# A causal mask that moves from two GpSimd products to a bfloat16 product in PSUM, in one head group of a two-layer hybrid decoder

## The chip, the cores and the metric

The kernel runs on one core of a Trainium2 chip. TensorE (PE in the rows) does matrix products and transposes, VectorE (DVE) elementwise work and scans, ScalarE (ACT) activations and copies, GpSimd (POOL) elementwise work and the DMAs with indices, SyncE (SP) issues the other DMAs. Each engine takes its instructions in the order in which the built program has them. The metric is the device time of one execution in microseconds, and lower is better.

## The reference

The model has two layers. In each a token mixer with four head groups (A to D, four heads of 64 each) reads one shared projection, and a mixture of experts follows. The change is in group B, stick-breaking attention over 1024 tokens in blocks of 128 queries:

```python
for i in range(S // SB_BLOCK):
    q0 = i * SB_BLOCK
    kl = q0 + SB_BLOCK
    z = jnp.einsum('bqhd,bkhd->bhqk', q[:, q0:kl], k[:, :kl]).astype(F32) * scale
    t_idx = q0 + jnp.arange(SB_BLOCK)[:, None]
    s_idx = jnp.arange(kl)[None, :]
    mask = s_idx < t_idx
    log1m = jnp.where(mask, jax.nn.log_sigmoid(-z), 0.0)
    cs = jnp.cumsum(log1m, -1)
    log_a = jax.nn.log_sigmoid(z) + cs[..., -1:] - cs
    att = jnp.where(mask, jnp.exp(log_a), 0.0)
    outs.append(jnp.einsum('bhqk,bkhd->bqhd', att.astype(v.dtype), v[:, :kl]))
```

Only the last 128 of a block's `kl` keys, the diagonal block, are touched by the mask: there a query sees the keys before it and not itself.

## The kernel before

A layer has four stages: the input projection; the mixers with the output projection; a short end in which the last tiles are normed and routed; and the experts, whose weights stream in from memory. The program's text weaves generators (one for each head group, one for the output projection `outs`), and an automatic scheduler then fixes each engine's order by its own estimates. So a change of one head group's instructions moves the others' too.

Group B is the class `Stick`. One `unit` is one block of 128 queries of one head: 8 blocks, 4 heads and 2 layers make 64 units. Two units (the heads h = 0 and 1 of a pair) are stepped in turn, and three pairs of tiles `z` and `e` go round. A unit does this:

1. TensorE makes the scores in PSUM tile `a`, in pieces of up to 512 keys, with two products for each piece (`sk` and `sq` in the rows), and VectorE copies each piece to `z`, cut at 40 (L574).
2. ScalarE makes exp and then ln(1 + x) of it in `e`.
3. GpSimd multiplies the diagonal block of `e` by a mask of ones and zeros (L579).
4. VectorE sums `e` from the right (the scan, L580) and subtracts it from `z` (L582); ScalarE takes exp of `z`.
5. GpSimd multiplies the diagonal block of `z` by the same mask (L584).
6. TensorE transposes `z` (L148, `cst` is the identity), ScalarE or VectorE copies that to `e`, and the products with the values (`sv`) add into PSUM tile `b`.

At the end of four blocks `head_norm` norms the result `yb` (L551). RWKV (group A) runs in the same stretch; `tl`, `ra`, `mp`, `ya` are its tiles, and its last instruction of a piece is L503. GpSimd also works for it (L392, L412) and for the output projection (L2078, L2140). A helper records all matrix products as L143 and all activations as L160.

Of the kernel before, what the change touches and what calls it, by code (L numbers as in the profile page):

```python
# [12 lines left out]
BF16 = mybir.dt.bfloat16  # L13
# [4 lines left out]
ALU = mybir.AluOpType  # L18
# [4 lines left out]
P = 128  # L23
# [26 lines left out]
def const_table():  # L50
    p = np.arange(P)
    s, t = p[:, None], p[None, :]
    parts = []

    def put(name, a):
        a = np.asarray(a, np.float32)
        b = np.zeros((P, a.shape[1]), np.float32)
        b[:a.shape[0]] = a
        CONST_COLS[name] = (sum(x.shape[1] for x in parts), a.shape[1])
        parts.append(b)  # L60

    put("ident", np.eye(P))
    put("rep64", (p[:, None] % 64 == np.arange(64)[None, :]))
    put("blk64", (s // 64 == t // 64))
    u, v = p[:, None] % 64, np.arange(64)[None, :]
    put("mp4", np.concatenate([u < v, u <= v, u < v, u <= v], 1))
    put("su", s < t)
    put("sl", t < s)
    put("dneg", np.where(t <= s, 0.0, NEG))
    put("mneg", np.where(s <= t, 0.0, -30000.0))  # L70
    put("ep", np.concatenate([np.arange(4)[:, None] == (p[None, :] // 64 + 2 * j) for j in range(2)], 1))
    put("tokid", np.stack([2 * (128 * k + p) + c + 1 for k in range(NT) for c in range(2)], 1))
    put("iota", np.broadcast_to(p[None, :], (P, P)))

    lev = lambda b: (s // (2 * b) == t // (2 * b)) & (s % (2 * b) < b) & (t % (2 * b) >= b)
    put("lev", np.concatenate([lev(1 << l) for l in range(6)], 1))
    return np.concatenate(parts, 1)
# [11 lines left out]


CONSTS = const_table()
NCONST = CONST_COLS["lev"][0]


class K:


    def __init__(self, ctx, tc, nbig, nmed, consts_dram):
        self.tc, self.nc, self.n = tc, tc.nc, 0
        self.ctx = ctx  # L100
        self.bigp = ctx.enter_context(tc.tile_pool(name="big", bufs=nbig))
        self.medp = ctx.enter_context(tc.tile_pool(name="med", bufs=nmed))
        self.cp = ctx.enter_context(tc.tile_pool(name="cp", bufs=1))
        self.sp = ctx.enter_context(tc.tile_pool(name="sp", bufs=2))
        self.ps = ctx.enter_context(tc.tile_pool(name="ps", bufs=1, space=PSUM))
        self.cst = self.cp.tile([P, NCONST], F32, name="cst")
        self.nc.sync.dma_start(self.cst, consts_dram[:, 0:NCONST])
        t = self.big("lev", 768)
        self.nc.sync.dma_start(t, consts_dram[:, NCONST:NCONST + 768])
        self.lev = self.cp.tile([P, 768], BF16, name="levb")  # L110
        self.nc.vector.tensor_copy(self.lev, t)
        self.evn, self.pe = 0, 0.0
        self.mode, self.mode_load, self.mode_acts = None, None, []
# [440 lines left out]
class Stick:  # L554


    def __init__(self, k, pc):
        self.k, self.pc = k, pc
        self.qk, self.y, self.done = {}, {}, set()

    def unit(self, i, h, py, own):
        k, nc = self.k, self.k.nc
        V, G = nc.vector, nc.gpsimd
        hs = slice(64 * (h % 2), 64 * (h % 2) + 64)
        q, kt = self.qk[i // 4, h // 2]
        q = q[:, 512 * (h % 2) + 128 * (i % 4):512 * (h % 2) + 128 * (i % 4) + 128]
        kl = 128 * (i + 1)
        z, e = own
        for o in range(0, kl, 512):
            n = min(512, kl - o)  # L570
            pz = k.psum("a", n)
            k.mm(pz, q, kt[h % 2][0][:, o:o + n], stop=False)
            k.mm(pz, q, kt[h % 2][1][:, o:o + n], start=False)
            V.tensor_scalar(z[:, o:o + n], pz, 40.0, None, op0=ALU.min)  # L574
        k.act(e[:, :kl], z[:, :kl], AF.Exp)
        k.act(e[:, :kl], e[:, :kl], AF.Ln, bias=1.0)
        yield
        dg = slice(kl - 128, kl)
        G.tensor_tensor(e[:, dg], e[:, dg], k.c("sl"), op=ALU.mult)  # L579
        V.tensor_tensor_scan(e[:, :kl][:, ::-1], e[:, :kl][:, ::-1], e[:, :kl][:, ::-1], initial=0.0,  # L580
                             op0=ALU.add, op1=ALU.bypass)
        V.tensor_tensor(z[:, :kl], z[:, :kl], e[:, :kl], op=ALU.subtract)  # L582
        k.act(z[:, :kl], z[:, :kl], AF.Exp)
        G.tensor_tensor(z[:, dg], z[:, dg], k.c("sl"), op=ALU.mult)  # L584
        yield
        at = e
        for o in range(0, kl, 512):
            n = min(512, kl - o)
            pt = k.psum("a", n)
            for b in range(n // 128):  # L590
                k.tr(pt[:, 128 * b:128 * b + 128], z[:, o + 128 * b:o + 128 * b + 128])
            k.ev(at[:, o:o + n], pt)
        if not py:
            py.append(k.psum("b", 128))
        for b in range(i + 1):
            k.mm(py[0][hs], self.v[:, b, hs], at[:, 128 * b:128 * b + 128],
                 start=b == 0, stop=b == i)
        yield
# [1018 lines left out]
class Trunk:  # L1617
# [12 lines left out]
    def setup(self):  # L1630
        k, nc, ins = self.k, self.nc, self.ins
        V, G, cp = nc.vector, nc.gpsimd, k.cp
        cr = k.big("crow", 128)
        G.memset(cr, 0.0)
        nc.scalar.dma_start(cr[0:8], ins["c"].rearrange("o (n p) -> (o n) p", p=P))
        self.raw = k.big("prow", 128)
        G.memset(self.raw, 0.0)
        for l in range(L_LAYERS):
            for n, cnt in PARAM_ROWS:
                src = ins[PARAM_IN[n]][l]  # L1640
                src = src.rearrange("t (n p) -> (t n) p", p=P) if n == "cw" else src.rearrange("(n p) -> n p", p=P)
                o = 64 * l + PARAM_OFF[n]
                nc.gpsimd.dma_start(self.raw[o:o + cnt], src)

        pt = k.psum("b", 128)
        k.tr(pt, cr)
        cs = k.small("cs", 16, bufs=1)
        k.act(cs[:, 0:8], pt[:, 0:8], AF.Sigmoid)
        V.tensor_tensor(cs[:, 8:16], cs[:, 0:8], pt[:, 0:8], op=ALU.mult)
        self.cz = cp.tile([P, 8, 32], F32, name="cz")  # L1650
        G.memset(self.cz, 0.0)
        V.tensor_copy(self.cz[:, :, 0], cs[:, 8:16])
        self.eps = k.eps = cp.tile([P, 2], F32, name="eps")
        G.memset(self.eps[:, 0:1], 1e-6)
        G.memset(self.eps[:, 1:2], 64e-5)
        self.rst = cp.tile([P, S], BF16, name="rst")
        G.memset(self.rst, 1.0)
        self.one = cp.tile([P, P], F32, name="one")
        G.memset(self.one, 1.0)
        G.memset(self.rst.rearrange("p (c l) -> p c l", l=64)[:, :, 0], 0.0)  # L1660
        self.sums = cp.tile([P, 2, P], BF16, name="sums")
        V.tensor_copy(self.sums[:, 0], k.c("su"))
        G.memset(self.sums[:, 1], 1.0)
        self.idb = cp.tile([P, P], BF16, name="idb")
        V.tensor_copy(self.idb, k.c("ident"))
        self.mneg4 = cp.tile([P, 4, P], BF16, name="mneg4")
        V.tensor_copy(self.mneg4, k.c("mneg").unsqueeze(1).to_broadcast([P, 4, P]))
        self.zd = cp.tile([P, 256], F32, name="zd")
        G.memset(self.zd[:, 0:128], 0.0)
        V.tensor_copy(self.zd[:, 128:256], k.c("dneg"))  # L1670
# [276 lines left out]
    def layer(self, l):  # L1947
        k, nc, ins = self.k, self.nc, self.ins
        pc = self.pc(l)
# [30 lines left out]
            yield from ds.scores()  # L1980
            yield from ds.search()

        sb = Stick(k, pc)
        sb.eps = self.eps[:, 0:1]
        stage = set()
        until = lambda f: iter(lambda: None if f() else WAIT, None)
# [204 lines left out]
```

## Time and profile before

| | us |
|---|---|
| median of 3 runs | 3679.66 (3675.84 to 3692.8) |
| the profiled execution, its time | 3683.57 |
| the profiled execution, its span on the core | 3681.8 |
| TensorE busy in the span | 3226.8 (88%) |
| VectorE busy | 2779.7 (75%) |
| ScalarE busy | 1934.4 (53%) |
| GpSimd busy | 845.3 (23%) |

The span runs from the first to the last instruction; the time lies 1.8 us above it. Busy is the time in which an engine works on an instruction. A share over the whole span is a mean over stages with different limits, so it says little of one stage.

### The profile page before, as it was taken

Reading aid. Unit: us, or ns where it says so; the run is one execution under the profiler, and the core shown is the slowest. Engines: PE = TensorE matmul, PEld = TensorE weight load, DVE = VectorE, ACT = ScalarE, POOL = GpSimd, SP = SyncE. Lnnn points to the kernel's source line nnn. Section 1 sums busy time; section 2 is a strip of 40 time slices with the busy share of each in tenths; the row PEclk is TensorE's granted clock in tenths of the full one; section 3 lists DMA queues with packets and bytes.
Section 4 is the critical chain, followed back from the end, with each engine's and each line's share of the span. In section 5 each row is a group of like instructions: output and inputs, shape, how many; then the busy total and the mean of one; then the engine's idle time right before and its main releaser. Section 6 shows DMA issues by size and latency. Waiting matters only on the chain. (4 is left out here: it accounts for less than half of the span.)

```text
span 3681.8 us, 54634 instructions
## 1 busy us (share of the span) xinstructions
PE 3226.8 (88%) x18838; PEld 2535.1 (69%) x18848; DVE 2779.7 (75%) x5556; ACT 1934.4 (53%) x3324; POOL 845.3 (23%) x769
## 2 busy tenths in 40 slices
PE   6888889998888799999958888999888879999995
PEld 3876645576677678777757866767667667877773
DVE  4589843557766899999856997555776679999994
ACT  4456332234444567777753663433444456777773
POOL 3220110113322113322312102011332211432220
PEclk8989999999988899999979989989998889999997
DMA  5222355533434899999931233023343389999995
GB/s 195 76 85 89 117 192 193 170 125 99 134 115 154 273 371 381 381 382 387 341 110 58 90 97 101 14 76 125 101 132 115 137 282 366 381 382 382 388 347 167
DMA packets 373670, 746.60 MB, mean 203 GB/s; under 512 B 44234, under 2 KB 108384, under 8 KB 373392
## 3 DMA queue, kind: packets, MB, share of 16 engines
q1 hardware_dynamic: 346880, 672.03, 50.9%
q0 software_dynamic: 20256, 70.33, 7.3%
q8 instruction: 149, 2.44, 0.3%
q10 hardware_dynamic: 6256, 0.74, 0.1%
q14 instruction: 129, 1.06, 0.1%
HBM read 635.45 MB, written 107.53 MB: 202 GB/s over the span
## 5 line engine op out<-in xcount | busy, mean ns | idle before, releaser
L160 ACT ACTIVATE wh<-wr 128x1024 fp32r<-128x1024 f32 (+3 forms) x900 | 887.4, 1005 | 328.1 <-DMA wr<-in_moe_w_dram 162.8
L1529 DVE TENSOR_TENSOR wl<-wr,wh 128x1024 fp32r<-128x1024 f32 x792 | 938.1, 1222 | 67.9 <-ACT wh L160 58.8
L143 PE MATMUL pj<-wl,xh 128*128 128x512 f32 x1056 | 419.5, 404 | 15.4 <-DVE wl L1529 14.8
L143 PE MATMUL pj<-wh,xh 128*128 128x512 f32 x1056 | 422.2, 401 | 9.0 <-ACT xh L160 8.4
L143 PE MATMUL pj<-wh,xl 128*128 128x512 f32 x1056 | 420.2, 398 | 0.0
L143 PEld LDWEIGHTS pj<-wl,xh 128*128 128x128 f32 x1056 | 200.1, 190 | 84.4 <-DVE wl L1529 41.1
L143 PEld LDWEIGHTS pj<-wh,xh 128*128 128x128 f32 x1056 | 200.1, 190 | 54.8 <-ACT xh L160 11.0
L143 PEld LDWEIGHTS pj<-wh,xl 128*128 128x128 f32 x1056 | 200.7, 190 | 46.8 <-DVE xl L1541 1.7
L1428 POOL DMA_INDIRECT xg<-h2d,si x64 | 76.6, 1198 | 632.1 <-PE a L148 370.3
L143 PE MATMUL b<-wh,hh 128*128 128x512 f32 x528 | 211.3, 401 | 10.7 <-ACT wh L160 9.1
L143 PE MATMUL pj<-hh,wh 128*128 128x512 f32 x480 | 197.1, 411 | 14.7 <-ACT wh L160 5.7
L143 PE MATMUL b<-wh,hl 128*128 128x512 f32 x528 | 209.2, 396 | 0.0
L143 PE MATMUL pj<-hh,wl 128*128 128x512 f32 x480 | 195.9, 408 | 7.7 <-DVE wl L1845 7.7
L143 PE MATMUL pj<-wh,hh 128*128 128x256 f32 (+2 forms) x640 | 187.2, 305 | 16.9 <-DVE stl L1962 11.5
L143 PE MATMUL pj<-wh,hl 128*128 128x256 f32 (+2 forms) x640 | 192.7, 303 | 3.2 <-DVE hl L1822 3.2
L143 PE MATMUL pj<-hl,wh 128*128 128x512 f32 x480 | 194.1, 404 | 0.0
L143 PE MATMUL pj<-wl,hh 128*128 128x256 f32 (+2 forms) x640 | 189.0, 298 | 2.5 <-POOL wl L1845 2.5
L160 ACT ACTIVATE ra<-b 128x256 f32<-128x256 f32 x192 | 73.2, 383 | 216.1 <-PE b L143 213.8
L143 PE MATMUL b<-wl,hh 128*128 128x512 f32 x528 | 176.8, 411 | 2.2 <-DVE wl L1529 2.1
L1498 POOL DMA_INDIRECT xs<-yo,si x32 | 146.8, 4588 | 124.9 <-DVE yo L1495 111.0
L1498 POOL DMA_INDIRECT out_dram<-yo,si x32 | 136.3, 4259 | 135.7 <-DVE yo L1495 117.1
L421 DVE TENSOR_TENSOR tl<-pj,tl 128x512 f32<-128x512 f32 x128 | 87.1, 685 | 94.7 <-PE pj L143 93.8
(523 smaller groups left out, 7794.5 us busy)
## 6 DMA issues: line engine op xcount, KB each, us to landing
wr<-in_moe_w_dram SPq DMA_DIRECT2D x792, 512.0 KB
aw<-in_ada_w_dram SPq DMA_DIRECT2D x96, 512.0 KB
wr<-in_w_in_dram SPq DMA_DIRECT2D x84, 256.0 KB
wo<-in_w_out_dram SPq DMA_DIRECT2D x48, 256.0 KB
xs<-xp SPq DMA_DIRECT2D x48, 256.0 KB
xp<-xs SPq DMA_DIRECT2D x48, 256.0 KB
out_dram<-xp SPq DMA_DIRECT2D x48, 256.0 KB
sk<-pt SPq DMA_DIRECT2D x32, 256.0 KB
```

What stands on the lines that cost most here:

```text
L143: return self.nc.tensor.matmul(out, lhsT, rhs, start=start, stop=stop, skip_group_check=True)
L160: i = self.nc.scalar.activation(out, in_, f, **kw)
L421: V.tensor_tensor(tt, pT, tt, op=ALU.add)
L1428: self.k.nc.gpsimd.indirect_dma_start(out=xg, out_offset=None, in_=self.h2d, in_offset=bass.IndirectOffsetOnAxis(ap=gi.bitcast(U32), axis=0))
L1498: k.nc.gpsimd.indirect_dma_start(out=self.xs, out_offset=bass.IndirectOffsetOnAxis(ap=si.bitcast(U32), axis=0), in_=yo, in_offset=None, co ...
L1529: i = nc.vector.tensor_tensor(wl, raw, wh.bitcast(F32), op=ALU.subtract)
```

## The change

A constant `low`, 0 where a query may see a key and -30000 elsewhere, takes the place of the mask of ones and zeros. It is cast to bfloat16 once at the start. In each unit a third product, `low` as the weights against a bfloat16 identity, adds it to the diagonal block of the scores while they are in PSUM. Behind exp, ln(1 + x), the sum and the second exp the masked places are then 0 by themselves, and both GpSimd products are gone.

```diff
-    put("sl", t < s)
+    put("low", np.where(s < t, 0.0, -30000.0))
...
             k.mm(pz, q, kt[h % 2][0][:, o:o + n], stop=False)
-            k.mm(pz, q, kt[h % 2][1][:, o:o + n], start=False)
+            last = o + n == kl
+            k.mm(pz, q, kt[h % 2][1][:, o:o + n], start=False, stop=not last)
+            if last:
+
+                k.mm(pz[:, n - 128:], self.low, self.idb, start=False)
             V.tensor_scalar(z[:, o:o + n], pz, 40.0, None, op0=ALU.min)
         k.act(e[:, :kl], z[:, :kl], AF.Exp)
         k.act(e[:, :kl], e[:, :kl], AF.Ln, bias=1.0)
         yield
-        dg = slice(kl - 128, kl)
-        G.tensor_tensor(e[:, dg], e[:, dg], k.c("sl"), op=ALU.mult)
         V.tensor_tensor_scan(e[:, :kl][:, ::-1], e[:, :kl][:, ::-1], e[:, :kl][:, ::-1], initial=0.0,
                              op0=ALU.add, op1=ALU.bypass)
         V.tensor_tensor(z[:, :kl], z[:, :kl], e[:, :kl], op=ALU.subtract)
         k.act(z[:, :kl], z[:, :kl], AF.Exp)
-        G.tensor_tensor(z[:, dg], z[:, dg], k.c("sl"), op=ALU.mult)
         yield
...
+        self.low = cp.tile([P, P], BF16, name="low")
+        V.tensor_copy(self.low, k.c("low"))
...
-        sb = Stick(k, pc)
+        sb = Stick(k, pc, self.low, self.idb)
```

The scheduler makes a new order of it. The first place is TensorE's order at the first units of layer 0; before, the scores of two units stood together:

```order
L143 MATMUL a_7584<-sk_7567,sq_7566 128x128 x2
L143 MATMUL a_7618<-sk_7574,sq_7566 128x128 x2
L148 MATMUL a_7642<-cst,z_7560 128x128
L143 MATMUL b_7645<-e_7561,sv_7581 64x128
L143 MATMUL b_7647<-tl_4464 128x128 x2
```

The same place of the change:

```order
L143 MATMUL a_7586<-sk_7569,sq_7568 128x128 x2
L143 LDWEIGHTS low
L143 MATMUL a_7586<-idb,low 128x128
L143 MATMUL a_7621<-sk_7576,sq_7568 128x128 x2
L143 LDWEIGHTS low
L143 MATMUL a_7621<-idb,low 128x128
L148 MATMUL a_7642<-cst,z_7562 128x128
```

Each unit has a load of weights and a product more, and nothing else changes place here. In 62 of the 64 units the new product stands directly behind the scores; in the other two a few other products lie between.

The second place is TensorE's order around the last two units of layer 0 (block 7, the last two heads): first before, from the last transpose of the pair ahead of them.

```order
L148 MATMUL a_10211<-cst,z_7562 128x128
L143 MATMUL b_10106<-rp_10036,st_9807 64x64 x2
L143 MATMUL a_10239<-sk_9710,sq_9709 128x512
L143 MATMUL a_10239<-sk_9711,sq_9709 128x512
...
L143 MATMUL b_10117<-ya_7433,cst 128x256
L143 MATMUL b_10122<-sqh_10120,cst 128x256
L143 MATMUL b_10128<-gd_7190,lw_291 128x256
L143 MATMUL b_10173<-e_7561,sv_9726 64x128 x7
L143 MATMUL b_10173<-e_7563,sv_9726 64x128 x7
L143 MATMUL b_10195<-wr_304,h2t_10181 128x36 x8
```

And the same place of the change, where `wr` and `h2t` are the router's product, and `sqh`, `gd` are of RWKV's output:

```order
L148 MATMUL a_10198<-cst,z_7564 128x128 x3
L143 MATMUL b_10096<-sqh_10094,cst 128x256
L143 MATMUL b_10102<-gd_7192,lw_293 128x256
L143 MATMUL b_10145<-e_7563,sv_9731 64x128 x7
L143 MATMUL b_10145<-e_7565,sv_9731 64x128 x4
L143 MATMUL b_10167<-wr_306,h2t_10153 128x36 x8
L143 MATMUL b_10145<-e_7565,sv_9731 64x128 x3
L143 MATMUL a_10211<-sk_9715,sq_9714 128x512
L143 MATMUL a_10211<-sk_9716,sq_9714 128x512
```

The scores of the last two units stood ahead of the 14 value products of the pair before them and now stand behind these and the router's product.

The third place is ScalarE's order at these last two units; before, they work in `z_7564` and `z_7560`:

```order
L160 ACTIVATE e_7565<-z_7564 128x1024
L160 ACTIVATE e_7565<-e_7565 128x1024
L160 ACTIVATE sqh_10120<-ya_7433 128x256
L160 ACTIVATE sqh_10120<-b_10122,eps 128x256
...
L160 ACTIVATE sqh_10120<-sqh_10120 128x256
...
L160 ACTIVATE e_7561<-z_7560 128x1024
```

The same place of the change, where they work in `z_7566` and `z_7562`:

```order
L160 ACTIVATE sqh_10094<-b_10096,eps 128x256
L160 ACTIVATE sqh_10094<-sqh_10094 128x256
...
L160 ACTIVATE e_7567<-z_7566 128x1024
L160 ACTIVATE e_7567<-e_7567 128x1024
L160 ACTIVATE e_7563<-z_7562 128x1024
L160 ACTIVATE e_7563<-e_7563 128x1024
```

The second unit's first exp stood behind three activations of RWKV's output and now follows the first unit's directly.

## Rows read from the trace of the kernel before

**Rows 1.** Busy time by stretch: start:end in us, length, then each engine's busy us.

```profile
core 0: us, PE busy (x) PEld busy (x) DVE busy (x) ACT busy (x) POOL busy (x), PEclk, DMA share, GB/s
828.00:1146.00 318.00, 270.01 (x2233) 216.73 (x2232) 223.85 (x407) 145.91 (x319) 93.02 (x120) 0.91 0.38 114
2578.00:2901.00 323.00, 270.42 (x2217) 218.87 (x2216) 225.95 (x406) 144.77 (x317) 95.64 (x119) 0.90 0.37 113
```

**Rows 2.** L503 (RWKV) and L551 (Stick), 828 to 1200: min/median/max ns, first and last start.

```profile
L503 DVE TENSOR_TENSOR ya<-sqh,b x5: 389/412/422, 895.9 to 1128.6; 128x256 f32<-128x256 f32 x5
L551 DVE SCALAR_TENSOR_TENSOR yb<-yb,prm,sqh x4: 744/752/1252, 900.0 to 1144.6; 128x512 f32<-128x512 f32 x4
```

**Rows 3.** GpSimd's two groups with the mask: busy us, mean ns, idle before.

```profile
L584 POOL TENSOR_TENSOR z<-z,cst 128x128 f32<-128x128 f32 x64 | 41.9, 656 | 130.0 <-ACT z L160 130.0
L579 POOL TENSOR_TENSOR e<-e,cst 128x128 f32<-128x128 f32 x64 | 31.7, 499 | 180.3 <-ACT e L160 153.6 <-DMA sq<-pt 26.6
```

**Rows 4.** Who waited for these two lines, whole span: us in total, times.

```profile
  DVE e L580: 13.8, 23
  PEld b L143: 1.5, 2
  PEld a L148: 19.1, 12
  PE a L148: 16.7, 12
```

**Rows 5.** Timeline around 2643 us: start, us, instruction, idle before it and releaser.

```profile
2642.87 0.30 ACT L160 ACTIVATE e<-e 128x128 f32<-128x128 f32 x1
...
2643.25 0.46 POOL L579 TENSOR_TENSOR e<-e,cst 128x128 f32<-128x128 f32 x1 [0.51 <-ACT e L160]
...
2643.74 1.48 DVE L580 TENSOR_TENSOR_SCAN e<-e 128x128 f32<-128x128 f32 x1 [0.39 <-POOL e L579]
```

**Rows 6.** Waits of DVE, then of PE, 828 to 1146: us in total, times, longest.

```profile
DVE e L580 <- POOL e L579: 7.7, 12, 1.7
...
PE a L148 <- POOL z L584: 8.4, 6, 6.1
```

**Rows 7.** Wide and narrow weight loads and products of TensorE: min/median/max ns, or mean.

```profile
L143 PEld LDWEIGHTS <-idb x16: 95/96/253, 653.1 to 2562.5; 128*128 128x128 bf16 x16
L143 PE MATMUL a<-sk,sq 128*128 128x128 f32 x32 | 6.9, 278 | 1.0 <-ACT yc L160 0.7
```

**Rows 8.** VectorE's scan and difference by shape: busy us, mean ns.

```profile
L580 DVE TENSOR_TENSOR_SCAN e<-e 128x128 f32<-128x128 f32 x8 | 7.6, 946 | 2.4 <-POOL e L579 2.4
L580 DVE TENSOR_TENSOR_SCAN e<-e 128x256 f32<-128x256 f32 x8 | 6.4, 804 | 0.9 <-POOL e L579 0.9
L582 DVE TENSOR_TENSOR z<-z,e 128x768 f32<-128x768 f32 x8 | 9.5, 1191 | 0.0
L582 DVE TENSOR_TENSOR z<-z,e 128x896 f32<-128x896 f32 x8 | 8.5, 1077 | 0.0
```

**Rows 9.** Timeline of the last two units of layer 0.

```profile
1118.32 0.33 PE L148 MATMUL a<-cst,z 128*128 128x128 f32 x1
...
1119.61 0.69 DVE L574 TENSOR_SCALAR z<-a 128x512 f32<-128x512 f32 x1 [0.96 <-PE a L143]
...
1122.05 0.69 DVE L574 TENSOR_SCALAR z<-a 128x512 f32<-128x512 f32 x1
...
1122.35 1.06 ACT L160 ACTIVATE e<-e 128x1024 f32<-128x1024 f32 x1
...
1125.02 2.89 PE L143 MATMUL b<-e,sv 128*64 128x128 f32 x28
...
1126.80 1.06 ACT L160 ACTIVATE e<-z 128x1024 f32<-128x1024 f32 x1 [0.88 <-PE b L143]
...
1127.84 1.98 PE L143 MATMUL b<-wr,h2t 128*128 128x36 f32 x16
...
1136.05 1.09 PE L148 MATMUL a<-cst,z 128*128 128x128 f32 x8
```

More of the change, by code (lines that the diff above doesn't have):

```diff
@@ L554, with __init__ @@
 class Stick:
-    def __init__(self, k, pc):
+    def __init__(self, k, pc, low, idb):
         self.k, self.pc = k, pc
+        self.low, self.idb = low, idb
         self.qk, self.y, self.done = {}, {}, set()
@@ L562, in unit @@
         k, nc = self.k, self.k.nc
-        V, G = nc.vector, nc.gpsimd
+        V = nc.vector
         hs = slice(64 * (h % 2), 64 * (h % 2) + 64)
```

## The prediction

> **What bounds the kernel now.** I read the busy time by stretch first, to find where group B works and which engine is nearest its limit there. Group B's 64 units run in two stretches, one for each layer, of 318 and 323 us. In them TensorE works 270 us of each, VectorE some 225, ScalarE some 145, GpSimd 93 to 96 [rows 1]. So no engine is full: TensorE is at 84 to 85%, and the rest is waits between engines that each take their instructions in a fixed order. GpSimd is far from a limit, so what it is relieved of is worth nothing as work. It can only be worth something as a wait.
>
> Next I read when the two streams of the stretch end. In layer 0 the last norm of group B starts at 1144.6, the last piece of RWKV at 1128.6 [rows 2]. Group B ends last, so a shorter group B can shorten the stretch. All before and behind it (projection, norms, experts) is the same work and moves with the end.
>
> Then the two mask lines by themselves and who waited for them. They are 128 products, 73.6 us of GpSimd in all, 0.46 to 0.66 us each [rows 3]. Waits that end at them: VectorE's scan 23 times, 13.8 us; TensorE's transposes 12 times, 16.7 us (19.1 us seen from the weight loads, which is the same wait); a product with values twice, 1.5 us [rows 4]. So of 128 products only some 37 were waited for at all. The other 91 were hidden, since their consumer was held up by something else or had other work ahead.
>
> **The change, part by part.**
>
> *The two GpSimd products go.* What one costs the waiting engine I take from the timeline: ScalarE's ln ends at 2643.17 (2642.87 and 0.30), GpSimd runs from 2643.25 to 2643.71, and the scan starts at 2643.74 [rows 5]. A direct hand-over from ScalarE to VectorE stays and costs about the 0.08 us that ScalarE to GpSimd took. That leaves at most 0.49 us for each wait.
>
> - Scan: 23 waits of at most 0.49 us would be 11.3 us. The mean wait is 0.6, but the longest is 1.7 [rows 6], so others are shorter than 0.49. I take 0.4 each, 9 us, between 0 and 11.3.
> - Transposes: the longest wait in layer 0 is 6.1 of 8.4 us [rows 6], and 16.7 is twice 8.4, so I take layer 1 to have the same. In these two TensorE waits for a whole unit's chain, and the product is 0.49 of it. The other ten sum to 16.7 - 12.2 = 4.5 us. Together 4.5 + 1.0 = 5.5.
> - Product with values: two waits, 1.5 us in all, of which 2 x 0.49, about 1.0, is the mask's.
>
> Not all of this reaches the end. What TensorE gains (6.5 us) I count whole, since it is nearest to full. Of the 9 us of VectorE I count half, because VectorE is idle 30% of the stretch [rows 1] and often runs into the next wait instead. Gain 11 us; the ends are 0 and 17.8 (11.3 + 5.5 + 1.0).
>
> *VectorE is less disturbed.* The scan of 128 columns takes 946 ns, more than that of 256 at 804; the difference of 768 columns takes 1191, more than that of 896 at 1077 [rows 8]. What holds up a form that is slower than a wider one is not its size; GpSimd, working beside it in the same memory, is what I suspect. At 0.5 to 0.8 us the narrow scan would give back 1.1 to 3.6 us over its 8, and at 0.92 (1077 x 768 / 896) the difference 2.2 us. That is 3 to 6 us of VectorE, of which other GpSimd work (L412, L392, L2078) causes a part. I take 2 us, between 0 and 6.
>
> The Trainium skill bears on this row ("SBUF — State Buffer", "Who interferes with whom"): a VectorE instruction with two inputs in SBUF shares a read port with a GpSimd instruction that reads SBUF, and whichever starts first holds it for its whole length while the other blocks. By that rule the slow forms would be wholly the mask's where no other GpSimd work is near, and the sum would come out up to 4 us lower, at 3669. These rows agree with the direction and can't split the blame.
>
> *The product with the mask comes.* The trace has no product of 128 columns in bfloat16. Two rows bound it. The bfloat16 identity's weight load takes 96 ns, and the product behind it should be about hidden under the next load; a product of 128 columns of the scores lasts 278 ns alone, with its drain [rows 7]. Below nothing is excluded, as it is added work. Since 62 of 64 stand between other products in TensorE's order, where only the spacing counts, I take 0.096: 64 x 0.096 = 6.1 us, of which the 85% that TensorE is busy counts, 5.2 us. The upper end is 64 x 0.278 = 17.8. Behind the added product waits the copy of the scores (L574), and behind that the unit's exp; that delay is inside the same price. The cast of `low` at the start is one VectorE instruction of 128 columns, below the 0.69 us of a 512-column copy [rows 9], beside the first loads: 0.
>
> *The order of the last two units changes.* The scores start now behind the pair's value products and the router's. Before, the last transpose ended at 1118.65 and the first copy of scores began at 1119.61, 0.96 later. Now a copy of the transposes (0.69, as wide a copy), the value products (2.89) and the router's (1.98) lie between, 5.6 us, so 4.6 later. But the second unit's first exp, which began at 1126.80 behind RWKV's activations, could follow the first unit's ln, which ended at 1123.41 [rows 9]: 3.4 earlier, and 0.5 more for the product that the first unit no longer waits for. Net 0.7 us later in each layer, 1.4 in all. The second unit's transposes, at 1136.05, are late next: they then depend on VectorE's two scans alone.
>
> *Sum.* -11 - 2 + 5.2 + 1.4 = -6.4 us. The profiled execution took 3683.57, which would become 3677.2. It lies 3.9 us above the median of the three runs, so against the median I forecast 3679.66 - 6.4 = 3673.
>
> **The rivals.**
>
> *Group B's own chain sets the pace.* If in nearly all steps a pair of units goes through both links one after the other, 32 pairs x 2 x 0.49 = 31 us come off, less 5.2 for the new products: 3654. For it: group B ends last [rows 2], and TensorE has 48 to 53 us of idle time in each stretch [rows 1]. Against it: only 37 of 128 products were seen to be waited for [rows 4]. A hidden product may still have shaped the order that the scheduler chose.
>
> *The new product costs as much as a lone one.* It stands between the scores and their copy, where the copy waits for its drain. At 278 ns [rows 7] and with only TensorE's own 6.5 us coming back, 17.8 + 1.4 - 6.5 = 12.7 us are lost: 3692. It decides from 0.24 us a product, where 64 x 0.85 x 0.24 equals the 13 us of the gains. For it: TensorE is the busiest engine. Against it: 62 of 64 stand in a row of products. A new order elsewhere that fits worse would add to it.
>
> *Nothing moves.* The waits at GpSimd turn into waits at ScalarE of the same length, because ScalarE's exp was only just done; the new products fill idle time. Then 3680. For it: in the two longest waits all but 0.49 of 6.1 us is the rest of the unit's chain. Against it: 0.49 us is a clean piece of each link [rows 5].
>
> **How the numbers follow.** About 0.5% (18 us) is what a measurement of this kernel can tell from no change. Chances: my forecast 0.43, the chain 0.27, the dear product 0.18, nothing 0.12. Faster by over 0.5% (below 3661) is the chain's case, 0.27. Of the dear product's 0.18 I give 0.11 to beyond 3698, with a worse order; that is slower. The rest is 0.62. The range reaches from 3650, somewhat under the chain's time, to 3695, over that of the dear product: it leaves out the far part of either, about 0.1 each. The forecast's own range, from the ends of its terms (gains 17.8 and 6, the product's spacing at 5.2; or gains 6.5 and the product at 17.8 x 0.85), is 3662 to 3690.
>
> **What would show it.** In the profile after: no L579 or L584 of GpSimd, and GpSimd's busy time 70 to 75 us lower. Scans that wait for ScalarE's `e`, 0.3 to 0.5 us shorter than they waited for GpSimd. The first units' long waits of TensorE, 6.1 us, about 5.6. The weight load of `low` near 96 ns and its product with a spacing below 0.1. The narrow scan below 0.8 us and the 768 difference near 0.92. Both stretches 2 to 5 us shorter, and all other stages the same. It is wrong if the stretches shrink by 10 us or more each (the chain), if TensorE's busy time there grows by more than 8 us a layer (the dear product), or if a stage without group B moves.

## The result, and the profile after

| | us |
|---|---|
| before, median of 5 runs | 3687.42 (3675.84 to 3692.8) |
| after, median of 5 runs | 3711.65 (3707.91 to 3713.87) |
| after to before | 1.0072, 95% interval 1.006 to 1.0085 |

The change makes the kernel slower by 0.7%, some 25 us. The forecast was 3673, range 3650 to 3695, with 0.11 for slower. The first line of the page after, busy time of each engine in a span of 3712.0:

```profile
PE 3240.9 (87%) x18912; PEld 2546.7 (69%) x18912; DVE 2782.0 (75%) x5557; ACT 1937.9 (52%) x3324; POOL 777.8 (21%) x641
```

GpSimd lost 67.5 us, and the span still grew by 30. The two stretches of group B in the change, as in [rows 1]; their ends are moved with the events:

```profile
828.00:1167.00 339.00, 279.55 (x2261) 225.23 (x2260) 225.40 (x408) 146.78 (x319) 61.98 (x54) 0.87 0.34 106
2597.00:2932.00 335.00, 277.09 (x2240) 223.10 (x2240) 222.25 (x404) 146.22 (x316) 57.63 (x51) 0.88 0.35 105
```

They are 21 and 12 us longer (318 and 323 before). All else only moves along. TensorE is busy 9.5 and 6.7 us more, at a lower granted clock (0.91 and 0.90 before). The last pieces of RWKV and of group B in layer 0, as in [rows 2]:

```profile
L503 DVE TENSOR_TENSOR ya<-sqh,b x5: 407/411/421, 891.4 to 1137.0; 128x256 f32<-128x256 f32 x5
...
L551 DVE SCALAR_TENSOR_TENSOR yb<-yb,prm,sqh x4: 735/740/1148, 896.8 to 1165.1; 128x512 f32<-128x512 f32 x4
```

The first ones start 3 to 5 us earlier than before, as the forecast had it. The last ones start 8 and 20 us later, and group B now ends 28.1 us behind RWKV instead of 16.0. So something between 900 and 1165 costs more than the whole gain.

What was forecast of the single operations is there. The weight load of `low`, and its product:

```profile
L143 PEld LDWEIGHTS <-low x64: 95/96/146, 839.8 to 2910.5; 128*128 128x128 bf16 x64
L143 PE MATMUL a<-idb,low x64: 219/230/330, 839.8 to 2910.5; 128*128 128x128 bf16 x64
```

VectorE's scan and difference by shape in layer 0, as in [rows 8]:

```profile
L585 DVE TENSOR_TENSOR z<-z,e 128x768 f32<-128x768 f32 x4 | 4.1, 1020 | 0.0
...
L583 DVE TENSOR_TENSOR_SCAN e<-e 128x128 f32<-128x128 f32 x4 | 2.2, 545 | 0.0
```

The scan of 128 columns takes 545 ns here and 416 in layer 1, where it took 946 in both. The difference of 768 takes 1020 in both, where it took 946 in layer 0 and 1437 in layer 1 (1191 in the mean).

### The profile page after: what moved, and what is told of

Same layout as the page of the kernel before. It is cut to its first block, busy times and chain, and to the rows that moved or that the text cites. A ratio compares the mean times of both kernels' runs of the same rounds, so it can differ in the third digit from the quotient of the medians.

```text
span 3712.0 us, 54714 instructions
## 1 busy us (share of the span) xinstructions
PE 3240.9 (87%) x18912; PEld 2546.7 (69%) x18912; DVE 2782.0 (75%) x5557; ACT 1937.9 (52%) x3324; POOL 777.8 (21%) x641
## 5 line engine op out<-in xcount | busy, mean ns | idle before, releaser
L143 PE MATMUL pj<-hh,wh 128*128 128x512 f32 x480 | 198.3, 414 | 13.7 <-ACT wh L160 7.0
L143 PE MATMUL pj<-wh,hh 128*128 128x256 f32 (+2 forms) x640 | 186.3, 303 | 17.2 <-DVE stl L1967 10.6
L392 POOL TENSOR_TENSOR tl<-mp,levb 128x256 f32<-128x256 f32 x64 | 57.6, 921 | 526.3 <-DVE mp L380 496.0
```

What stands on the lines that cost most here:

```text
L143: return self.nc.tensor.matmul(out, lhsT, rhs, start=start, stop=stop, skip_group_check=True)
L392: G.tensor_tensor(four(ml[i]), l2, lv(i + 1), op=ALU.mult)
```

## What else the change moves

The program's text is woven by a rule that the forecast did not look at. `K.mm` counts the columns of every product, and `weave` lets the stream go on that is furthest behind by this count:

```python
self.pe += n / 2400 * (4 if rhs.dtype == F32 else 1)    # K.mm
...
s[0] += (k.pe - before + (other or 0.2)) / pace         # weave
```

The mask product counts 128 / 2400 = 0.053 in each unit, so group B's stream seems to be further on than before, and RWKV's stream is written earlier against it. No stream moves by more than four steps, but 138 of the 368 steps of RWKV's stream do move. The scheduler takes the text's order as priority, and tile buffers are handed out in that order too, so each engine gets another order.

## Experiments

Below, "uncounted" is the change with the count taken back behind the product. Each run's median stands with its ratio to the kernel before, taken on the same chip (whose median was 3684.6 to 3687.4).

**Is it the order, the product, or the removal?** e1 is the change uncounted, e2 the kernel before with the count alone and not one instruction more:

```diff
 # e1: the change
                 k.mm(pz[:, n - 128:], self.low, self.idb, start=False)
+                k.pe -= 128 / 2400
 # e2: the kernel before
             k.mm(pz, q, kt[h % 2][1][:, o:o + n], start=False)
+            if o + n == kl:
+                k.pe += 128 / 2400
```

e3 is e1 without the mask product, so it leaves the mask out; with other data the routing to the experts differs, and only its mixer stretches can be read. e4 is e1 with GpSimd's two products kept.

> The changed kernel, but the weave that interleaves the head groups' text doesn't count the mask product's 128 columns, so that the text stands in the order of before; the scheduler still orders anew. Order theory (the loss of 24 us comes from the new order of the other work): the time comes back to near that of before, 3675 to 3690. Product theory (the added TensorE product costs it): as the change, 3705 to 3715. Removal theory (without GpSimd's delay the units crowd the others): as the change, 3705 to 3715.

> The kernel before with one thing added that makes no instruction: the weave counts 128 columns more for each unit, as it does in the change. Order theory, if the weave's count makes the bad order: slower by 10 to 30 us, 3697 to 3715. Product theory and removal theory: as before, 3680 to 3692, since no instruction is added or taken away.

> Leaves the mask out altogether: neither the GpSimd products nor the TensorE product. Order theory: 3670 to 3690, since the text's order is that of before. Product theory: 10 to 15 us under before, 3672 to 3678. Removal theory: as slow as the change, 3700 to 3715.

> The mask twice: the GpSimd products stay and the TensorE product is added, uncounted by the weave. Order theory: 3685 to 3700, the price of the products (about 5 us) and what the scheduler makes of it. Product theory: 3705 to 3715 or more. Removal theory: as before plus about 5, 3690 to 3697.

| run | us | ratio, 95% |
|---|---|---|
| e1_uncounted | 3675.37 | 0.9968 (0.9957 to 0.9979) |
| e2_count_only | 3734.36 | 1.0135 (1.0111 to 1.0159) |
| e3_no_mask | 3677.39 | 0.9976 (0.9963 to 0.999) |
| e4_both | 3684.03 | 0.9999 (0.9987 to 1.0011) |

The count alone costs the kernel before 48 us. Taking it back gains the change 36 us and makes it faster than before. Both masks together, uncounted, cost nothing that can be told from noise. So the loss is the order's.

**Where is it lost?** For this I matched each instruction of TensorE, VectorE, ScalarE and GpSimd with that of the kernel before, by its line, its tiles and its turn, and took the median shift of those within 6 us of a mark. The table has the growth of the shift between marks (times of the kernel before), from one profile of each kernel:

| run | 940 to 1055 | 1055 to 1165 | 2690 to 2805 | 2805 to 2920 |
|---|---|---|---|---|
| the change | +13.9 | +10.5 | +11.1 | +5.8 |
| e16, the change again | +14.0 | +10.3 | +10.9 | +5.7 |
| e2 (count alone) | +11.5 | +19.6 | +12.7 | +10.1 |
| e1 (uncounted) | +4.1 | +0.7 | +3.8 | -3.7 |
| e5 (blocks 0 to 3) | +13.7 | +3.8 | +10.6 | -1.0 |
| e6 (blocks 4 to 7) | +2.9 | +1.2 | +3.0 | -2.7 |
| e15, e6 again | +4.9 | +3.3 | +2.3 | -2.6 |
| e7 (-128 columns) | +5.5 | +4.7 | +3.5 | +1.5 |
| e8 (256 columns) | -0.3 | +12.1 | -0.4 | +6.1 |
| e9 (the change, stores last) | +5.0 | +11.4 | +7.0 | +5.5 |
| e10 (64 columns) | +12.8 | +3.2 | +2.1 | 0.0 |
| e11 (-64 columns) | +7.8 | +7.5 | +6.3 | -3.6 |
| e17, e9 again | +7.3 | +13.3 | +7.4 | +5.4 |
| e18 (e5, stores last) | +6.3 | -1.1 | +12.1 | +6.8 |

From 828 to 940 the kernels without GpSimd's products gain 2 to 7 us on that before, all but e7 and e11. The change and e2 lose at the same two places of each layer: where block 4 of group B begins, and at the stretch's end. Nearly the same numbers in a second profile (e16) say that this is no scatter.

**Which part of the count does it?** Four counts, each a line behind the product in place of e1's:

```diff
+                k.pe -= 128 / 2400 * (i > 3)    # e5: counted in blocks 0 to 3 only
+                k.pe -= 128 / 2400 * (i < 4)    # e6: counted in blocks 4 to 7 only
+                k.pe -= 256 / 2400              # e7: counts as minus 128
+                k.pe += 128 / 2400              # e8: counts as 256
```

> The change, with its mask products counted by the weave in blocks 0 to 3 of group B only. Place theory (the loss of the change is made where group B comes late to one place: its first pair of block 4 reaches TensorE some 6 us later just when RWKV goes from one trio of units to the next, at 955 to 1005 us; a second, smaller loss follows at the stretch's end): group B is as late at block 4 as in the change, so +12 to +16 us against the uncounted change (3675) near 1005 in layer 0, the same in layer 1, and 3695 to 3705 in all, with less lost at the end than the change lost. Lottery theory (each new text order gives another order of the engines, and its price has nothing to do with where group B is late): anything from 3665 to 3735, with the losses in other places.

> The change, with its mask products counted in blocks 4 to 7 only. Place theory: the text up to 940 us is that of the uncounted change, so there is no loss at 955 to 1005; at the stretch's end 0 to 8 us a layer, so 3675 to 3691. Lottery theory: 3665 to 3735 all the same.

> The change, with each mask product counted as minus 128 columns, so that group B's text comes earlier by about as many steps as it came later in the change. Place theory: group B is early at RWKV's change of trios, so no loss there: 3665 to 3680, faster than before. Lottery theory: as likely as dear as the change, 3690 to 3735.

> The change, with each mask product counted as 256 columns. Place theory: group B is later still at the change of trios, at least what the change lost: 3710 to 3745, with +14 us or more against the uncounted change near 1005. Lottery theory: may as well be 3670 to 3700.

| run | us | ratio, 95% |
|---|---|---|
| e5_first_half | 3696.74 | 1.0019 (1.0009 to 1.0029) |
| e6_second_half | 3667.5 | 0.9951 (0.9933 to 0.9969) |
| e7_early | 3695.23 | 1.002 (1.0009 to 1.0031) |
| e8_double | 3687.89 | 1.0006 (0.9991 to 1.0021) |

The halves came out as the place theory said: the count of blocks 0 to 3 alone brings the first place's loss, that of blocks 4 to 7 none. The other two speak against it: minus 128 columns is no gain, and 256 columns lose nothing at block 4. So being late there does not set the price by itself; that it is how the pieces happen to fit is not shown.

**What happens at that place?** SyncE's queue in e1 (start, us, line, transfer): stores of the output projection (`xs<-xp`), its next weights (`wo`), and group B's queries and keys for block 4 (`sq`, `sk`):

```profile
915.92 15.17 SPq L2131 DMA_DIRECT2D xs<-xp  x4
931.14 0.92 SPq L2083 DMA_DIRECT2D wo<-in_w_out_dram  x2
937.79 0.33 SPq L2131 DMA_DIRECT2D xs<-xp  x1
938.17 0.45 SPq L637 DMA_DIRECT2D sq<-pt  x1
938.66 1.24 SPq L637 DMA_DIRECT2D sk<-pt  x2
```

The same in the change:

```profile
918.61 23.53 SPq L2130 DMA_DIRECT2D xs<-xp  x6
942.19 0.93 SPq L2082 DMA_DIRECT2D wo<-in_w_out_dram  x2
943.16 0.45 SPq L636 DMA_DIRECT2D sq<-pt  x1
943.66 1.23 SPq L636 DMA_DIRECT2D sk<-pt  x2
```

A store waits on SyncE until its sum is made. Ahead of the output projection's weights stand six stores now, where four stood in e1 and before, and the weights issue 11 us later than in e1. Ahead of group B's loads stand six, where five stood, and these issue 5 us later. The timeline of the change shows who pays (PE and PEld, TensorE; DVE, VectorE; `pj<-ar` and `mp`, RWKV's next three units):

```profile
954.16 0.23 PE L143 MATMUL a<-idb,low 128*128 128x128 bf16 x1
...
954.58 0.39 PE L143 MATMUL pj<-ar,ks 64*64 64x128 f32 x4
...
958.66 0.87 PE L143 MATMUL a<-sk,sq 128*128 128x512 f32 x2 [3.69 <-issue]
...
959.46 0.69 PE L143 MATMUL pj<-ar,kn 64*64 64x128 f32 x4
...
960.63 0.42 DVE L380 TENSOR_TENSOR mp<-pj,cst 128x256 f32<-128x256 f32 x1 [5.11 <-PE pj L143]
...
961.20 1.72 POOL L392 TENSOR_TENSOR tl<-mp,levb 128x256 f32<-128x256 f32 x1 [13.46 <-DVE mp L380]
```

TensorE stands 3.69 us at the scores of block 4, and RWKV's products, which need no key, stand behind them in its order. VectorE waits 5.11 us for these. The profile names no releaser; that it is the keys is shown by e17 below. The same place as a stretch, before, then in the change, then in e1 (columns as in [rows 1], ends moved with the events):

```profile
940.00:1060.00 120.00, 102.81 (x889) 82.87 (x888) 85.75 (x143) 51.99 (x105) 33.74 (x41) 0.91 0.51 141
```

```profile
937.00:1071.00 134.00, 110.03 (x901) 88.99 (x900) 88.70 (x147) 54.72 (x110) 24.63 (x23) 0.83 0.46 130
```

```profile
936.00:1060.00 124.00, 102.16 (x896) 82.98 (x895) 90.89 (x147) 54.57 (x109) 25.18 (x23) 0.93 0.48 135
```

Against e1 the place is 10 us longer. Of these, 7.9 are TensorE being busy longer over as many products (901 and 896), and 2.1 are idle. So what the place loses against e1 is mainly the granted clock. It stood at 1.00 until the stall and fell in it: from 955 to 960 TensorE is busy 27%, at a mean of 0.72. In slices of 25 us the change has

```profile
960.00:985.00 25.00, 19.90 (x129) 14.70 (x125) 17.48 (x30) 7.43 (x13) 6.48 (x6) 0.70 0.24 76
985.00:1010.00 25.00, 18.56 (x95) 13.15 (x95) 19.97 (x30) 14.09 (x27) 5.72 (x4) 0.70 0.32 105
1010.00:1035.00 25.00, 17.88 (x110) 16.05 (x110) 17.58 (x23) 8.01 (x15) 7.96 (x9) 0.76 0.31 105
```

and e1

```profile
960.00:985.00 25.00, 20.43 (x155) 14.77 (x154) 19.74 (x37) 10.37 (x20) 5.50 (x6) 0.86 0.15 50
985.00:1010.00 25.00, 14.55 (x92) 11.66 (x93) 21.29 (x28) 13.63 (x25) 10.03 (x8) 0.80 0.56 185
1010.00:1035.00 25.00, 23.31 (x176) 20.71 (x175) 18.03 (x21) 9.25 (x16) 6.17 (x7) 1.00 0.55 138
```

A mean of 0.70 to 0.76 over 75 us says that TensorE ran at 1.2 GHz for about half of it, where e1 was back at 2.4 GHz from 1010 on. How much of this is the stall's own, e17 shows below.

**Is it SyncE's queue?** e9 is the change with the last two stores put behind the loads; the order tie binds SyncE's own queue alone. In the built order some 15 of TensorE's 15,000 rows, 22 of VectorE's 5,300 and 16 of ScalarE's 3,100 stand elsewhere too; at the wait itself TensorE's order is that of the change:

```diff
-                nc.sync.dma_start(self.xs[l][t, ns], x)
+                if js[0] == 4 and n == 1 and i in tiles[-2:]:
+                    k.held.append((self.xs[l][t, ns], x))
+                else:
+                    nc.sync.dma_start(self.xs[l][t, ns], x)
...
-            k.nc.sync.dma_start(self.v, ...)
+            d = k.nc.sync.dma_start(self.v, ...)
+            while k.held:
+                st = k.nc.sync.dma_start(*k.held.pop(0))
+                k.order(getattr(st, 'ins', st), getattr(d, 'ins', d))
```

e10 and e11 count the product as 64 and as minus 64 columns. e17 is e9 once more, and e18 makes e9's edit on e5.

> The change as it is; the last two stores of the output projection's part that stands ahead (xs<-xp) are put behind its next weight loads and group B's loads for block 4 on SyncE's queue, where six stores stood ahead of these loads against four before. The orders of the other engines stay but for some 20 rows of 15,000 on TensorE. Queue theory (block 4 is late since its loads wait behind two more stores): the loads issue 6 to 10 us earlier and the 14 us that layer 0 lost between 940 and 1060 come back, and as much in layer 1: 3684 to 3692. Order theory (TensorE's own order holds the scores of block 4 behind some 80 rows of RWKV, whenever their data come): 0 to 4 us come back in a layer, 3703 to 3712.

> The change, with the mask product counted as 64 columns. In the built order TensorE has RWKV's last products of a trio in a bunch there (38 and 24 rows with nothing of group B between), as in the change (45 and 35) and not as in the uncounted one (20, 24 and 22 rows with scores of block 4 between). Order theory: 10 to 14 us lost between 940 and 1060 in layer 0, 3690 to 3710 in all. If the amount counted sets the price in proportion: 3693. If the price has nothing to do with this bunch: 3665 to 3690 as well.

> The change, with the mask product counted as minus 64 columns. In the built order TensorE has at this place, row for row, what the uncounted change has. Order theory: no loss there beyond the 4 us of the uncounted change, 3665 to 3682. In proportion with the minus 128 columns (3695): 3685.

> The program of e9_stores_last once more, with more executions. Queue theory: 3693 to 3703, under the change (3712 to 3718) by the 13 us that its profile showed at the two places. If that profile was a lucky execution: 3705 to 3718, and the places lose again.

> The change counted in blocks 0 to 3 only (3696.7, with 13.7 and 10.6 us lost at the two places), with the last two stores of the output projection behind the loads on SyncE's queue. Queue theory: TensorE's wait of 4.1 us for block 4's scores and VectorE's of 5.5 us behind it go, 8 to 13 us come back in both layers together, 3683 to 3689. If the queue is not the cause: 3692 to 3701.

| run | us | ratio, 95% |
|---|---|---|
| e9_stores_last | 3712.65 (3695.65 to 3724.49, 4 runs) | 1.0078 (1.0048 to 1.0108) |
| e17_stores_again | 3703.84 (3696.74 to 3709.1, 6 runs) | 1.0046 (1.003 to 1.0062) |
| e10_half | 3696.82 | 1.0029 (1.0013 to 1.0045) |
| e11_minus_half | 3694.77 | 1.0024 (1.0013 to 1.0035) |
| e18_first_half_stores | 3701.32 | 1.0044 (1.0027 to 1.006) |

The loads of block 4 issue at 936.72 in e17, 7 us earlier, and TensorE's wait for the scores is gone. Their line in 940 to 975, the change first, with what its engine waited for:

```profile
L143 PE MATMUL a<-sk,sq x10: 223/431/794, 952.5 to 974.7; 128*128 128x512 f32 x6, 128*128 128x128 f32 x4
...
its engine sat idle before it (us, times) until:
  issue: 3.7, 1
```

```profile
L144 PE MATMUL a<-sk,sq x10: 220/438/793, 955.0 to 973.4; 128*128 128x512 f32 x6, 128*128 128x128 f32 x4
...
its engine sat idle before it (us, times) until:
who waited for it (us, times):
```

In e17, 6.7 of the 14.0 us come back at the first place and 3.5 of 10.9 in layer 1, against e16. At the end of layer 0's stretch 3.0 us more are lost. The first place of e17 as a stretch:

```profile
940.00:1067.00 127.00, 106.87 (x892) 86.11 (x891) 88.58 (x147) 54.26 (x110) 24.09 (x23) 0.87 0.46 129
```

It is 7 us shorter than in the change: TensorE is idle 3.8 us less and busy 3.2 us less. In e9, on another chip, these are 4.8 and 4.2 us. So the stall cost nearly as much in clock as in idle time. The 3 us that are left against e1 go with the clock: TensorE is idle 1.7 us less than in e1 and busy 4.7 us longer, at 0.87 against 0.93. The clock falls in e17 too, from 1.00 up to 965 to 0.62 in the next 5 us, behind another wait, which is longer now. In e17, then in the change:

```profile
963.89 0.33 PE L149 MATMUL pj<-cst,ar 128*128 128x128 f32 x1 [2.95 <-DVE xp L2114]
```

```profile
965.22 0.33 PE L148 MATMUL pj<-cst,ar 128*128 128x128 f32 x1 [1.06 <-DVE xp L2110]
```

The time of e17 is under that of e16 by 13.8 us. But e9's runs lie 29 us apart. Taken together by runs, e9 and e17 stand at 1.0059 of before and the change's two at 1.0079, some 7 us apart: a gain that is likely and not settled. On e5 the same edit takes the wait away as well and gives back 7.4 us at the place, and the time is not lower but 4.6 us higher: layer 1 loses more. And e8 has six stores ahead too, a wait of 1.9 us, and no loss there. So the queue is one cause at this place in the change, for about half of the loss, and no rule for other orders. e10 loses 12.8 us there with 1.2 us of that wait. e11 has, at the place, e1's rows on TensorE, and takes 19 us more than e1, most of it elsewhere; this part of the order theory fell.

**What are the operations worth, with the order held?** e12 and e13 are e4, in e4's order on every engine; behind the scheduling, each GpSimd product (e12) or each mask product (e13) is cut from 128 columns to 2. e14 is e4 once more, beside them:

```diff
+    for b in nc.main_func.blocks:
+        b.instructions = [i.__replace__(ins=[cut(x) for x in i.ins], outs=[cut(x) for x in i.outs])
+                          if i.name in narrow else i for i in b.instructions]
```

> The kernel with both masks (GpSimd's products and the product in PSUM, 3684), in exactly its order on every engine, with all 128 GpSimd products cut from 128 columns to 2 after the order was fixed; the product in PSUM does the whole mask. Terms of the forecast (each wait loses what GpSimd no longer does, 13 us in all with the share that a product of 2 columns keeps, estimated at a third): 6 to 10 us under the kernel with both at full size. Chain theory (31 us for the removal): 20 us under it. Order theory in its strict form (the removal is worth nothing, only the order counts): within 3 us of it.

> The same kernel with both masks, in exactly its order, with all 64 mask products in PSUM cut from 128 columns to 2; their weight loads stay, and GpSimd's products do the whole mask. Product at its spacing (5.2 us in all): 2 to 5 us under the kernel at full size. Product as a lone one (17.8 us): 10 us or more under it. Nothing: within 2 us.

> The kernel with both masks again, unchanged, as the measure for the two beside it: 3680 to 3690 by every theory.

| run | us | ratio, 95% |
|---|---|---|
| e12_narrow_gpsimd | 3685.84 | 0.9998 (0.999 to 1.0007) |
| e13_narrow_product | 3691.15 | 1.0008 (0.9998 to 1.0017) |
| e14_both_again | 3690.57 | 1.0013 (1.0 to 1.0026) |

GpSimd's products with 2 columns in e12, then with 128 in e14 (min/median/max ns):

```profile
L594 POOL TENSOR_TENSOR z<-z,cst x64: 188/196/2217, 845.8 to 2886.5; 128x2 f32<-128x2 f32 x64
L589 POOL TENSOR_TENSOR e<-e,cst x64: 194/196/923, 841.5 to 2881.4; 128x2 f32<-128x2 f32 x64
```

```profile
L591 POOL TENSOR_TENSOR z<-z,cst x64: 452/462/2478, 843.1 to 2893.6; 128x128 f32<-128x128 f32 x64
L586 POOL TENSOR_TENSOR e<-e,cst x64: 451/456/1442, 838.6 to 2888.2; 128x128 f32<-128x128 f32 x64
```

By the median they keep 43%; the means (395 and 288 ns of 677 and 544) are raised by single long ones. Cutting them gives 4.7 us in the medians, and in the profiles the two stretches together are 665 us instead of 674. Cutting the mask product gives nothing (+0.6 us). By the ratios' intervals, put together as roots of squares, the first gains 0 to 11 us and the second -4 to +8; the 20 us of the chain (31 x 0.57, some 18, by the share that really went) and the 10 us of a dear product are outside.

**Again.** e15 is e6's program, e16 the change.

> The program of e6_second_half once more. Its order is fast: 3664 to 3676 again, all under the kernel before. Picked from scatter: 3676 to 3690.

> The change itself once more, for a second profile. Place theory: between 940 and 1060 us of layer 0 and the same place of layer 1 again 10 to 14 us each are lost against the kernel before, and at the stretch's end again 5 to 10 us; 3705 to 3715. If the places were chance: the losses stand elsewhere in this profile, at the same sum.

e15 took 3670.11 (0.9954, 0.9941 to 0.9968), e16 3717.6 (1.0085, 1.0068 to 1.0102). The program of e6 is fast both times. It is the version that beats both kernels, the one before by 17 us and the change by some 45. Where it gains is not shown: its spans are 17 and 10 us shorter than that before, of which the stretches of group B make only 5 and 1; the rest lies mostly ahead of and between them, where the change's two executions differ by 4 us as well.

## Why the prediction was wrong, step by step

**The step that failed** is "The order of the last two units changes", with its 1.4 us, and the reading in front of it that nothing else changes place at the first units. The order was looked at in three places and priced in one. The product is counted by the weave, and the order changes throughout: worth 36 us between e1 and the change, 48 us alone (e2). The last two units did what was forecast: their two scans now start at 1144.62 and 1148.08, 3.5 us apart, where they started at 1123.97 and 1131.37, 7.4 apart. But the pair came 20.6 us later. Where the price could be traced, at the beginning of block 4, loads stood behind more stores on SyncE's queue than in e1, TensorE waited 3.7 us for them, and its granted clock fell.

**The two GpSimd products go (-11).** The direction was right, and the waits were about right where the order is held: from e14 to e12 the waits of the scans for GpSimd fall from 18.1 to 11.7 us and all waits of the transposes for GpSimd and ScalarE from 20.2 to 18.4, 8.2 us less for 57% of a product's time; 57% of the 9 and 5.5 us of the forecast are 8.3. In time that is 5 us in the medians (0 to 11) and 9 in the profiles. What was priced wrong is the first units' long wait, which was to shrink from 6.1 us to 5.6. It shrank to 2.9, in both layers. Before, GpSimd stood 13.3 us at the first mask product until its `e` was made (the profile names the load of the queries), and L2078, the output projection's weights, stood behind it in GpSimd's order. So L2078 ran just beside the scan:

```profile
842.04 0.77 POOL L579 TENSOR_TENSOR e<-e,cst 128x128 f32<-128x128 f32 x1 [13.32 <-DMA sq<-pt]
842.76 2.59 POOL L2078 TENSOR_TENSOR wo<-wo,mod 128x512 f32<-128x512 f32 x2
842.84 1.47 DVE L580 TENSOR_TENSOR_SCAN e<-e 128x128 f32<-128x128 f32 x1 [0.35 <-POOL e L579]
...
847.08 0.48 PE L148 MATMUL a<-cst,z 128*128 128x128 f32 x1 [6.06 <-POOL z L584]
```

In the change the same weights (L2083) are done long before:

```profile
828.20 2.49 POOL L2083 TENSOR_TENSOR wo<-wo,mod 128x512 f32<-128x512 f32 x2
...
841.92 0.42 DVE L583 TENSOR_TENSOR_SCAN e<-e 128x128 f32<-128x128 f32 x1
...
843.52 0.47 PE L148 MATMUL a<-cst,z 128*128 128x128 f32 x1 [2.91 <-ACT z L160]
```

The forecast had GpSimd's own work in the wait, and not what that work held up behind it.

TensorE's waits at the transposes and those of the scans in the change, 828 to 1167, beside [rows 6]:

```profile
PE a L148 <- ACT z L160: 12.0, 6, 6.1
...
DVE e L583 <- ACT e L160: 6.8, 7, 1.6
```

The kernel before had, beside the 8.4 us for GpSimd's `z`, this row for ScalarE's:

```profile
PE a L148 <- ACT z L160: 8.1, 3, 6.4
```

So the transposes wait 12.0 us where they waited 16.5, and 11.0 for 20.7 in layer 1. The scans wait 6.8 us for 7.7, and 4.5 for 6.1 in layer 1: in the change ScalarE took GpSimd's place there, as the third rival had it; in e1 only 5.9 us of the scans' 13.8 are left. The longest wait of the change, 6.1 us, is another one than before, at the last two units (1149 us).

**VectorE is less disturbed (-2, of 3 to 6 us of its time).** The size came out, the cause did not. The 8 scans of 128 columns take 0.47 us less (545 ns in layer 0, 416 in layer 1) and the 8 differences of 768 0.17 less, 5.1 us; those of 896 went the other way, by 0.14 each. But the mask's products were not what held them up. Of the 8 scans before, four take 1.47 to 1.48 us, and these run beside L2078, as above; the other four take 0.41 to 0.43, and two of these run beside a mask product for 0.1 us. The forecast gave other GpSimd work, L2078 among it, a part; it was all. In e12 the mask's products have 2 columns, L2078 still stands behind them, and the scan is as slow as before:

```profile
L590 DVE TENSOR_TENSOR_SCAN e<-e 128x128 f32<-128x128 f32 x8 | 7.6, 952 | 0.9 <-POOL e L589 0.4
```

Of the 768 differences one was slow, 2.9 us beside L2140, and that it fell elsewhere in the change is luck. GpSimd was what held up these forms, with work that was not the mask's. The Trainium skill's rule in "SBUF — State Buffer", "Who interferes with whom", that the two block each other at a shared port, agrees with this.

**The mask product (+5.2).** Its weight load takes 96 ns as forecast. Its columns cost nothing that can be seen (e13, which keeps the 64 loads), and both masks together stand at 0.9999 and 1.0013 of before (e4, e14), nothing to 5 us more. So the term is not refuted and looks rather too high; the lone price of 17.8 is out. The sign that was named for that rival, over 8 us more of TensorE in a stretch, did appear (9.5 in layer 0) and is no sign of it. The two stretches of e1 hold the same products, and TensorE is busy only 1.6 and 1.7 us more in them than before, at about the same clock:

```profile
828.00:1146.00 318.00, 271.65 (x2271) 219.89 (x2270) 223.94 (x407) 146.79 (x319) 61.87 (x56) 0.92 0.37 113
2578.00:2897.00 319.00, 272.12 (x2249) 220.71 (x2248) 226.77 (x407) 146.60 (x320) 60.76 (x54) 0.90 0.38 115
```

The rest of the 9.5 goes with the lower clock of the change (0.87).

**Forecasts of stages.** Both stretches were to be 2 to 5 us shorter; up to 940 layer 0 was, by 3, about what the first units' wait lost; e1 and e6 ended 0 to 4 us shorter in each, e15 3 longer and 4 shorter. That no stage without group B moves was right.

**The chance for slower** was 0.11, on the dear product with "a worse order" as its tail. The worse order was the whole case, and needed a rival of its own. What would have shown it was at hand: the difference of the built orders over the whole stretch, and the text's rule for weaving. I had read "a change of one head group's instructions moves the others' too" and priced it at two units.

**Open.** Why one order costs 3667 and another 3713 with the same instructions is explained at one place and for half of its loss; why the clock stays low there when the stall is gone is not shown. At the end of the stretch the change has group B alone for 28 us where before, e1, e5 and e15 have 16.0 (e2 36.4, e8 28.9); what makes it come late there was not tried by itself.

## What to carry to other kernels

Where the text's order is set by a cost count, an added instruction is also a change of that count: take it out of the count first and time both, before the instruction itself is judged. Here the operation was worth some 0.1 to 0.3% (e12, e1) and the order that came with it 1%. When such an order is up for choice, several nearby counts are cheap to try, and the fastest should be timed a second time, as e6 was.

On a queue that runs in order, look at what stands behind a store that waits for its data: a load that is ready to go may be what an engine two steps further on waits for. The same holds for an engine: an instruction that waits holds up the work behind it, and that work may then run where it disturbs another engine. Before a term is priced by the length of an instruction, look at what stands behind it.

## What the runs showed of the hardware

A GpSimd product of 2 columns takes 196 ns by the median, one of 128 columns 456 to 462 (e12, e14): some 40% of its price is not its size. GpSimd's spans are rough in the profile.

A VectorE scan of 128 columns takes 0.41 to 0.43 us, and 1.47 to 1.48 where it starts just behind a GpSimd product of 512 columns (the kernel before).

In the change a stall of 3.7 us on TensorE is followed by 75 us at a mean granted clock of 0.70 to 0.76. With the stall taken away (e17) the place has 3.8 us less idle time and 3.2 us less busy time over the same work, so each us of it cost nearly another one in clock. The rest of the low clock stays, behind another wait of 2.95 us.
